# Three edits to a two-block model on one core: who splits the output weights and when, 64-column block products, and key norms turned by transposition

## The chip, the cores and the metric

One Trainium2 chip, and on it one core. The metric is the device time of one execution in microseconds (us): the median of the runs shown.

## The reference, cut to what matters

The kernel computes a chain of layers on a sequence of 256 tokens of width 1024, in float32: a mixer of pooling and gated delta rule, an MLP, a spatial gating mixer, a second MLP, an RWKV-7 mixer, a third MLP, and a last norm. Two places of it are touched by the change.

```python
# first mixer (gated delta rule, 4 heads of width 128, chunks of 64): a unit triangular system per chunk
m = jnp.einsum('bhncd,bhnjd->bhncj', kb, kh) * decay_strict
sol = lax.linalg.triangular_solve(jnp.eye(C) + m, rhs, left_side=True, lower=True)
# RWKV-7 mixer (16 heads of width 64): the keys are scaled by their norm, and the result goes through w_o
kk = kk / jnp.maximum(jnp.sqrt(jnp.sum(kk * kk, axis=-1, keepdims=True)), 1e-12)
y = _wkv7_scan(r_h, heads(decay), k_h, v_h, kk, kk * heads(a))
...
return y @ w_o, v_first          # (256 x 1024) @ (1024 x 1024)
```

## The kernel before, in words

**Products in three parts.** A float32 matrix product of the projections is made of three fast ones. Each operand is split into a high part `h` (a cast to the rounded type `fp32r`) and a low part `l` (what the cast left out), and `mm3` adds `h h`, `h l` and `l h` (L225 to L227). A weight must therefore be loaded, cast and its low part made before its first use. `split` (L213, L217) casts on ScalarE (ACT) and subtracts on VectorE (DVE). With `lo="x"` it calls `rest` instead: ACT writes minus the high part into `l` (L221), and GpSimd (POOL) issues a DMA that adds the loaded weight onto it (L222). Small products inside the mixers are plain float32 matmuls; each shows in the trace as two weight loads and two matmuls, and a transposition as one of each.

**Order.** The library that builds the program orders each engine's queue itself, by its own estimates of durations, so a line's place in a queue isn't its place in the source. In the trace, TensorE (PE) runs matmuls of a later projection ahead of the key-norm matmuls that stand above it. Each queue is then worked off in order: an instruction that waits holds all that stand behind it on its engine. SyncE (SP) issues the weight loads, in the same way.

**First mixer** (`block1`). For two blocks `n` of 128 tokens and four heads, the inverse of a 128x128 triangular matrix is built by elimination in blocks of 16 and three doubling steps `b` = 16, 32, 64. Each step makes `Y = offT^T X` (L793), copies it to SBUF (ACT, L795), makes `Z = U^T Y` (L801) and `ZT = Y^T U` (L806), and adds them to `X` and `U` (DVE, L803 and L808). All are 128x128 per head. Between the steps, `fill()` lets pieces of other projections run.

**RWKV mixer** (`rwkv`). After the k, r and v projections, `scale_ab` (four calls) spreads the inverse key norms to 128x128 tiles (ACT, L1417) and multiplies each by the identity on PE (L1421), which turns it; DVE multiplies by the result (L1423). Then an elimination on DVE, and a scan over four windows `w` of 64 tokens for two halves `hb` of the heads. `step(s, fills)` works on window `s` of half 0 and window `s-1` of half 1: `state`, `solve`, `update`, `output`, each some small matmuls and an ACT copy out of PSUM (L1661, L1671, L1697). `fills` are four lists of other work that is put between them. Among it are `gate_in(n)` (loads `gb`, three DMAs), `gate(n, t)` (PE into `lg`, DVE), `fin(d, n)` (the norm of a finished half, on DVE and ACT, with transpositions into `yh`, `yl` at its end: L1705 to L1718, L246), `out_mm(t, k, first)` (the output product with weight chunk `k`, PE into `ra`), and `w_out`.

**Output weights.** Each call of `w_out` prepares the next of eight chunks `k` of 128 rows of `rwkv_w_o_2`. One load `rwo` of 1 MB holds two chunks. It lies in a "raw" buffer; there are two of these, which `gb`, the v weights ahead of it and the first loads of the third MLP (`m3u`, `m3d`) use too, in turn. Chunks 0 and 1 are split into buffers of the pool `wz` that the v weights used before. The other six go to homes that the scan frees on its way: chunk 2 to the tiles of the gain and of `sq`, 3 and 4 to `lv` (windows 0 and 1 of the scan's matrices), 5 to `EL`, 6 to `mix`, 7 to `lx` (window 2). All eight low parts are made by `rest`.

```python
if homes[k] is None:
    wo.append(split(w, "rwo", "x", of=wz))
else:
    h, l = homes[k]()
    act.copy(h, w)
    rest(l, h, w)
```

Of the kernel before, what the change touches and what calls it, by code (L numbers as in the profile page):

```python
# [10 lines left out]
F32 = mybir.dt.float32  # L11
# [6 lines left out]
P = 128  # L18
T = 256
# [105 lines left out]
def tile_two_blocks(ctx: ExitStack, tc: tile.TileContext, a: dict):  # L125
# [30 lines left out]
    def gps(name):  # L156
        turn[0] += 1
        if turn[0] % 4 < 2:
            return ps(name)
        if turn[1]:  # L160
            return lin(name)
        return acc(turn[0] % 4 - 2, name)[:, :512]
# [306 lines left out]
    def block1():  # L469
        with tc.tile_pool(name="b1", bufs=1) as bp, tc.tile_pool(name="b1s", bufs=2) as bs:  # L470
# [6 lines left out]
            with tc.tile_pool(name="n0", bufs=1) as np_:  # L477
# [20 lines left out]
                for i, (t, n) in enumerate(N_MAJOR if KP.get("um") else T_MAJOR):  # L498
# [3 lines left out]
                    if KP.get("uo") and i in KP["ui"]:  # L502
                        j = len(hl)
# [156 lines left out]
            def fill():  # L660
                n = KP["n"][step[0]]
                step[0] += 1
                for _ in range(n):
                    next(more, None)
# [49 lines left out]
            def v4(q):  # L714
                return q.rearrange("p (h c) -> p h c", h=4)
# [62 lines left out]
            for n in range(2):  # L778
# [7 lines left out]
                    pe.transpose(q[:, h * P:(h + 1) * P], X[:, n, h], ident)  # L786
                act.copy(U[:, n], v4(q))
            fill()
            for b in (16, 32, 64):
                for n in range(2):  # L790
                    q = gps("Y")
                    for h in range(4):
                        pe.matmul(q[:, h * P:(h + 1) * P], lhsT=offT[b][:, n, h], rhs=X[:, n, h],  # L793
                                  start=True, stop=True)
                    act.copy(Y[:, n], v4(q))  # L795
                fill()
                for n in range(2):
                    if b < 64:
                        q = gps("Z")
                        for h in range(4):  # L800
                            pe.matmul(q[:, h * P:(h + 1) * P], lhsT=U[:, n, h], rhs=Y[:, n, h],  # L801
                                      start=True, stop=True)
                        dve.tensor_add(X[:, n], v4(q), X[:, n])  # L803
                    q = gps("ZT")
                    for h in range(4):
                        pe.matmul(q[:, h * P:(h + 1) * P], lhsT=Y[:, n, h], rhs=U[:, n, h],  # L806
                                  start=True, stop=True)
                    dve.tensor_add(U[:, n], v4(q), U[:, n])  # L808
                fill()

            while not turn[1]:
# [329 lines left out]
    def rwkv(fed, early, cols, mu, hcol, hka, laf):  # L1141
        NP, CH = 8, 64
        half = 0.5 * DECAY
        with tc.tile_pool(name="wz", bufs=2) as wz, tc.tile_pool(name="rw", bufs=1) as bp:
# [75 lines left out]
            with tc.tile_pool(name="rwm2", bufs=2) as m2, tc.tile_pool(name="rwm", bufs=1) as mp:  # L1220
# [193 lines left out]
                def scale_ab(c):  # L1414
                    s = slice(2 * c, 2 * c + 2)
                    wide = wd[:, c].rearrange("p (t k n) -> p t k n", t=2, k=4)
                    act.copy(wide, nr[:, :, 4 * c:4 * c + 4].unsqueeze(3).to_broadcast([P, 2, 4, 64]))  # L1417
                    q = ps("nk")
                    for j in range(2):
                        for t in range(2):  # L1420
                            pe.matmul(q[:, j * T + t * P:j * T + t * P + P], rhs=ident, start=True, stop=True,  # L1421
                                      lhsT=wide[:, t, 2 * j:2 * j + 2].rearrange("p k n -> p (k n)"))
                    dve.tensor_tensor(out=tA[:, s], in0=tA[:, s], in1=as2(q.rearrange("p (j t) -> p j t", j=2)),  # L1423
                                      op=ALU.mult)
                    dve.scalar_tensor_tensor(tB[:, s], as2(ta[:, s]), -0.5, tA[:, s], ALU.mult, ALU.mult)
                    tA5 = tA[:, s].rearrange("p k d (e t) -> p k d e t", e=2)
                    EN[KP["tk"][0]].tensor_tensor(out=tA5, in0=tA5, in1=EL5[:, s, :, :, 0:CH], op=ALU.mult)
                    EN[KP["tk"][1]].tensor_tensor(out=tK[:, s], in0=tK[:, s], in1=as4(tt[:, s]), op=ALU.mult)
# [318 lines left out]
                def w_out():  # L1747
                    k = len(wo)
                    if k % 2 == 0:
                        wo_raw.append(load_as(a["rwkv_w_o_2"][0], k * P, f"rwo{k}"))  # L1750
                    w = wo_raw[-1][:, k % 2]
                    if homes[k] is None:
                        wo.append(split(w, "rwo", "x", of=wz))
                    else:
                        h, l = homes[k]()
                        act.copy(h, w)
                        rest(l, h, w)
                        wo.append((h, l))

                def out_mm(t, k, first):  # L1760
# [22 lines left out]
                for _ in c0:  # L1783
                    next(late_fill, None)
                before([(0, 0)])
                both_fill = [some(c1, 2) + some(late_fill, 2)] * 3
                step(0, both_fill + [rest_of(c1) + rest_of(late_fill) + [lambda: v_out(1), lambda: gate_in(0)]])
                yh, yl = xt_tiles("y")
                f00, f01, f10, f11 = [fin(d, n) for d in both for n in both]
                step(1, [[lambda: gate(0, 0)], [lambda: gate(0, 1), lambda: gate_in(1)], [w_out], [w_out]])  # L1790
                step(2, [some(f00) + [lambda: gate(1, 0)], some(f00) + [lambda: gate(1, 1)],
                         some(f00) + [w_out], some(f00)])
                step(3, [some(f01) + [w_out], some(f01) + [w_out], some(f01) + [w_out], some(f01) + [w_out, w_out]])
                ac = [acc(0, "ra0")]
                outs = lambda t, ks, first: [lambda k=k: out_mm(t, k, first) for k in ks]
                step(4, [some(f10) + outs(0, [0], 0), some(f10) + outs(0, [1], 0), [], some(f10) + outs(0, [2], 0)])
# [108 lines left out]
```

## Time and profile before

| What | us |
|---|---|
| median of 3 runs | 1082.83 (1080.8 to 1084.26) |
| the profiled execution's own time | 1082.16 |
| its span, first to last instruction | 1080.4 |

The span is 1.76 us shorter than the profiled execution's time, and that time lies 0.67 us under the median of the runs. PE is the busiest engine by far. A busy share is an average; where PE waits, and where its granted clock is down, is read stretch by stretch. PEld is PE's weight load, which runs beside its matmuls.

### The profile page before, as it was taken

The numbers are of one execution on the slowest core, as the hardware profiler recorded it, in microseconds if no ns is written. First come the engines' busy times: TensorE is split into PE (matmuls) and PEld (weight loads), VectorE is DVE, ScalarE is ACT, GpSimd is POOL, SyncE is SP. The second block draws the span as 40 slices with busy tenths as digits, with TensorE's granted clock in tenths as the row PEclk, the third lists the DMA queues.
The fourth block names the chain that finished last, engine by engine and source line by source line (L and its number), as shares of the span: only waits on it lengthen the run. The fifth ranks groups of instructions, "written<-read, shape, count | busy, mean of one in ns | idle before, by whom it ended". The sixth has DMA issues, their size and how long they took to land.

```text
span 1080.4 us, 18579 instructions
## 1 busy us (share of the span) xinstructions
PE 1043.5 (97%) x7626; PEld 932.3 (86%) x7626; DVE 716.3 (66%) x1201; ACT 567.3 (53%) x840; POOL 59.0 (5%) x94
## 2 busy tenths in 40 slices
PE   8999999999999999999999999999999789999996
PEld 6899878988899999889989998998777569999985
DVE  5989665555658886666685556998936465555565
ACT  5744464454456554555464546864656445444452
POOL 3100000000002000000000001022001100000000
PEclk9999999999999999999999999999999799999999
DMA  8343186555565645556575561456624874566531
GB/s 247 120 157 118 46 314 214 182 181 177 174 198 153 197 155 174 178 166 190 161 248 188 191 192 36 109 148 142 152 50 118 188 221 159 192 195 187 187 134 39
DMA packets 124465, 177.76 MB, mean 165 GB/s; under 512 B 6766, under 2 KB 100955, under 8 KB 124124
## 3 DMA queue, kind: packets, MB, share of 16 engines
q1 hardware_dynamic: 121930, 168.11, 49.0%
q0 software_dynamic: 2304, 8.39, 4.1%
q8 instruction: 60, 0.98, 0.4%
q14 instruction: 25, 0.20, 0.1%
q10 hardware_dynamic: 146, 0.07, 0.0%
HBM read 167.12 MB, written 1.05 MB: 156 GB/s over the span
## 4 chain that ended last, share of the span: by engine, by line
PE 82%; DVE 9%; DMA 4%; ACT 2%; issue 2%; POOL 1%; SPq 0%; ACTq 0%; POOLq 0%; DVEq 0%
PE m3h L227 3%; PE m3h L226 3%; PE m1a L225 3%; PE m3h L225 3%; PE m1a L227 3%; PE m1a L226 3%; PE m1h L226 3%; PE m2h L226 3%; PE m1h L227 3%; PE m2h L227 3%; PE m1h L225 3%; PE m2h L225 3%; PE m2a L225 3%; PE m2a L226 3%; PE m2a L227 3%; PE m3a L225 3%
## 5 line engine op out<-in xcount | busy, mean ns | idle before, releaser
L225 PE MATMUL m3h<-m3xh,m3uh 128*128 128x256 f32 x256 | 72.6, 284 | 1.9 <-ACT m3xh L382 1.9
L227 PE MATMUL m3h<-m3xh,m3ul 128*128 128x256 f32 x256 | 73.0, 285 | 0.5 <-DVE m3ul L217 0.5
L225 PE MATMUL m1h<-m1xh,m1uh 128*128 128x256 f32 x256 | 73.4, 287 | 0.0
L217 DVE TENSOR_TENSOR m3ul<-m3u,m3uh 128x1024 fp32r<-128x1024 f32 x32 | 39.2, 1226 | 51.1 <-ACT m3uh L213 51.1
L226 PE MATMUL m3h<-m3xl,m3uh 128*128 128x256 f32 x256 | 73.0, 285 | 0.0
L226 PE MATMUL m1h<-m1xl,m1uh 128*128 128x256 f32 x256 | 71.8, 281 | 0.2 <-DVE m1xl L385 0.2
L227 PE MATMUL m2h<-m2xh,m2ul 128*128 128x256 f32 x256 | 71.7, 280 | 0.0
L227 PE MATMUL m1h<-m1xh,m1ul 128*128 128x256 f32 x256 | 71.7, 280 | 0.0
L226 PE MATMUL m2h<-m2xl,m2uh 128*128 128x256 f32 x256 | 71.6, 280 | 0.0
L225 PE MATMUL m2h<-m2xh,m2uh 128*128 128x256 f32 x256 | 71.5, 280 | 0.0
L217 DVE TENSOR_TENSOR m1ul<-m1u,m1uh 128x1024 fp32r<-128x1024 f32 x32 | 39.2, 1225 | 45.1 <-ACT m1uh L213 45.0
L213 ACT CAST m3uh<-m3u 128x1024 fp32r<-128x1024 f32 x32 | 33.4, 1047 | 56.5 <-PE m3h L226 50.7
L217 DVE TENSOR_TENSOR m2ul<-m2u,m2uh 128x1024 fp32r<-128x1024 f32 x32 | 39.1, 1225 | 35.8 <-ACT m2uh L213 35.8
L213 ACT CAST m1uh<-m1u 128x1024 fp32r<-128x1024 f32 x32 | 33.7, 1053 | 52.3 <-PE m1h L226 50.5
L213 ACT CAST m2uh<-m2u 128x1024 fp32r<-128x1024 f32 x32 | 33.5, 1050 | 47.9 <-PE m2h L226 45.8
L217 DVE TENSOR_TENSOR m2dl<-m2d,m2dh 128x1024 fp32r<-128x1024 f32 x32 | 39.2, 1225 | 26.1 <-ACT m2dh L213 26.1
L217 DVE TENSOR_TENSOR m3dl<-m3d,m3dh 128x1024 fp32r<-128x1024 f32 x31 | 38.0, 1225 | 24.9 <-ACT m3dh L213 24.9
L217 DVE TENSOR_TENSOR m1dl<-m1d,m1dh 128x1024 fp32r<-128x1024 f32 x31 | 37.9, 1224 | 22.0 <-ACT m1dh L213 22.0
L225 PEld LDWEIGHTS m3h<-m3xh,m3uh 128*128 128x128 f32 x256 | 49.0, 192 | 2.8 <-ACT m3xh L382 2.2
L213 ACT CAST m2dh<-m2d 128x1024 fp32r<-128x1024 f32 x32 | 33.6, 1050 | 33.4 <-PE m2a L227 29.9
L213 ACT CAST m1dh<-m1d 128x1024 fp32r<-128x1024 f32 x31 | 32.5, 1047 | 35.3 <-PE m1a L227 24.4
L213 ACT CAST m3dh<-m3d 128x1024 fp32r<-128x1024 f32 x31 | 32.6, 1052 | 33.4 <-PE m3a L227 31.6
(691 smaller groups left out, 3513.4 us busy)
## 6 DMA issues: line engine op xcount, KB each, us to landing
m1u<-in_w_up_dram SPq DMA_DIRECT2D x16, 1024.0 KB, 5.5
m1d<-in_w_down_dram SPq DMA_DIRECT2D x16, 1024.0 KB, 5.0
m2u<-in_ffn_w_dram SPq DMA_DIRECT2D x16, 1024.0 KB, 6.4
m2d<-in_ffn_w_dram SPq DMA_DIRECT2D x16, 1024.0 KB, 5.2
m3u<-in_ffn_w_dram SPq DMA_DIRECT2D x16, 1024.0 KB, 5.5
m3d<-in_ffn_w_dram SPq DMA_DIRECT2D x16, 1024.0 KB, 5.1
win<-in_w_in_dram SPq DMA_DIRECT2D x10, 1024.0 KB, 5.3
sv<-in_sgu_w_in_dram SPq DMA_DIRECT2D x8, 1024.0 KB, 5.8
```

The lines of the kernel that those rows point to most:

```text
L213: act.copy(hv, src)
L217: lo.tensor_tensor(out=lv, in0=src, in1=hv.bitcast(F32), op=ALU.subtract)
L225: pe.matmul(out, lhsT=lh, rhs=rh, start=first, stop=False)
L226: pe.matmul(out, lhsT=lh, rhs=rl, start=False, stop=False)
L227: pe.matmul(out, lhsT=ll, rhs=rh, start=False, stop=last)
```

## The change

Four things are edited.

- `w_out` makes the low part of every chunk by one DVE subtraction in place of `rest` (`split` with its default, or `tensor_sub`). POOL's DMAs and ACT's second pass for these eight chunks are gone; the `rest` of the v weights stays.
- The calls of `w_out` are moved. Chunks 0 and 1 go from `step(1)` to the end of `step(0)`, right behind `gate_in(0)` and so ahead of `gate_in(1)`; chunk 2 from `step(2)` to `step(1)`; chunk 3 from `step(3)` to the end of `step(2)`; 4 to 7 stay in `step(3)`.
- The block products take 64 moving columns per head. `part` picks those columns of `X`, `Y` or `U` that are not zero or change, in pieces of `b` columns; the results lie packed in 256 columns of PSUM. The stationary operand stays 128x128. POOL now clears the other half of `Y` in each step.
- `scale_ab` uses a transposition where it multiplied by the identity.

```diff
             for b in (16, 32, 64):
                 for n in range(2):
+                    pool.memset(part(Y[:, n], b, 1), 0.0)
                     q = gps("Y")
                     for h in range(4):
-                        pe.matmul(q[:, h * P:(h + 1) * P], lhsT=offT[b][:, n, h], rhs=X[:, n, h],
-                                  start=True, stop=True)
-                    act.copy(Y[:, n], v4(q))
+                        pe.matmul(col64(q, h), lhsT=offT[b][:, n, h], rhs=part(X[:, n], b, 0, h), start=True, stop=True)
+                    act.copy(part(Y[:, n], b, 0), packed(q, b))
                 fill()
                 for n in range(2):
                     if b < 64:
...
-                            pe.matmul(q[:, h * P:(h + 1) * P], lhsT=U[:, n, h], rhs=Y[:, n, h],
-                                      start=True, stop=True)
-                        dve.tensor_add(X[:, n], v4(q), X[:, n])
+                            pe.matmul(col64(q, h), lhsT=U[:, n, h], rhs=part(Y[:, n], b, 0, h), start=True, stop=True)
+                        dve.tensor_add(part(X[:, n], b, 0), packed(q, b), part(X[:, n], b, 0))
...
-                        pe.matmul(q[:, h * P:(h + 1) * P], lhsT=Y[:, n, h], rhs=U[:, n, h],
-                                  start=True, stop=True)
-                    dve.tensor_add(U[:, n], v4(q), U[:, n])
+                        pe.matmul(col64(q, h), lhsT=Y[:, n, h], rhs=part(U[:, n], b, 1, h), start=True, stop=True)
+                    dve.tensor_add(part(U[:, n], b, 1), packed(q, b), part(U[:, n], b, 1))
...
-                            pe.matmul(q[:, j * T + t * P:j * T + t * P + P], rhs=ident, start=True, stop=True,
-                                      lhsT=wide[:, t, 2 * j:2 * j + 2].rearrange("p k n -> p (k n)"))
+                            pe.transpose(q[:, j * T + t * P:j * T + t * P + P],
+                                         wide[:, t, 2 * j:2 * j + 2].rearrange("p k n -> p (k n)"), ident)
...
-                        wo.append(split(w, "rwo", "x", of=wz))
+                        wo.append(split(w, "rwo", of=wz))
                     else:
                         h, l = homes[k]()
                         act.copy(h, w)
-                        rest(l, h, w)
+                        dve.tensor_sub(l, w, h.bitcast(F32))
...
-                step(0, both_fill + [rest_of(c1) + rest_of(late_fill) + [lambda: v_out(1), lambda: gate_in(0)]])
+                step(0, both_fill + [rest_of(c1) + rest_of(late_fill) + [lambda: v_out(1), lambda: gate_in(0), w_out, w_out]])
...
-                step(1, [[lambda: gate(0, 0)], [lambda: gate(0, 1), lambda: gate_in(1)], [w_out], [w_out]])
-                step(2, [some(f00) + [lambda: gate(1, 0)], some(f00) + [lambda: gate(1, 1)],
-                         some(f00) + [w_out], some(f00)])
-                step(3, [some(f01) + [w_out], some(f01) + [w_out], some(f01) + [w_out], some(f01) + [w_out, w_out]])
+                step(1, [[lambda: gate(0, 0)], [lambda: gate(0, 1), lambda: gate_in(1)], [w_out], []])
+                step(2, [some(f00) + [lambda: gate(1, 0)], some(f00) + [lambda: gate(1, 1)], some(f00), some(f00) + [w_out]])
+                step(3, [some(f01) + [w_out], some(f01) + [w_out], some(f01), some(f01) + [w_out, w_out]])
```

## Rows read from the trace of the kernel before

**Rows 1.** The page's first part: busy time of each engine, its share of the span, and its instructions.

```profile
PE 1043.5 (97%) x7626; PEld 932.3 (86%) x7626; DVE 716.3 (66%) x1201; ACT 567.3 (53%) x840; POOL 59.0 (5%) x94
```

**Rows 2.** Windows of the end of the RWKV mixer: each stretch and its length, busy time (instructions) of PE, PEld, DVE, ACT and POOL, then the granted clock of PE as a share of 2.4 GHz, the DMA share and GB/s.

```profile
821.00:833.00 12.00, 11.66 (x153) 10.03 (x152) 8.10 (x23) 7.71 (x11) 1.75 (x2) 1.00 0.58 131
833.00:848.00 15.00, 9.38 (x86) 6.83 (x85) 5.86 (x17) 8.37 (x11) 1.73 (x2) 1.00 0.81 176
848.00:867.00 19.00, 17.41 (x83) 12.79 (x81) 7.21 (x18) 9.35 (x14) 3.46 (x4) 0.55 0.81 193
867.00:878.40 11.40, 9.78 (x44) 7.29 (x44) 9.13 (x21) 3.46 (x6) 0.00 (x0) 1.00 0.79 253
878.40:889.00 10.60, 7.70 (x34) 5.45 (x34) 6.55 (x14) 6.15 (x16) 0.00 (x0) 1.00 0.72 228
```

**Rows 3.** The chain that ended last, in the stretch from 800 to 900 us, its longest pieces: start, us, what.

```profile
838.10 9.53 DMA lv<-rwo
859.87 10.59 DMA lx<-rwo
877.87 7.01 DMA m3u<-in_ffn_w_dram
```

**Rows 4.** The timeline around it: start, us, engine, line, what it writes from what it reads, and the idle time before it with what ended it.

```profile
840.13 0.92 PE L1693 MATMUL PD<-tBK,lx 128*64 128x64 f32 x13
845.23 1.04 ACT L1756 CAST lv<-rwo 128x1024 fp32r<-128x1024 f32 x1 [6.56 <-DMA rwo<-in_rwkv_w_o_dram]
847.67 0.50 PE L226 MATMUL ra<-lv,yh 128*128 128x512 f32 x1 [3.44 <-DMA lv<-rwo]
849.15 1.19 ACT L1697 COPY tBK<-PD 64x512 f32<-64x512 f32 x2
866.60 0.58 ACT L1697 COPY tBK<-PD 64x512 f32<-64x512 f32 x1 [0.67 <-PE PD L1693]
877.06 0.66 PE L246 MATMUL yt<-ident,tBK 128*128 128x128 f32 x4 [0.94 <-DVE tBK L1718]
```

**Rows 5.** What SP, which issues the loads, waited for between 740 and 900 us: us in total, times, longest. L184 loads `rwo` (and `m3d`), L1561 is the first load of a `gb`.

```profile
SPq L1561 <- DMA wvl<-wv: 30.5, 2, 16.7
SPq L184 <- DMA rwol<-rwo: 11.6, 1, 11.6
SPq L184 <- DMA lv<-rwo: 10.1, 1, 10.1
```

**Rows 6.** Costs of one split: groups between 805 and 890 us with total and mean ns (ACT's cast, ACT's second pass, a DVE subtraction of the same shape), and the last line of the tile `rwo`, the time to landing of the DMAs that read or write it.

```profile
L1756 ACT CAST wo<-rwo 128x1024 fp32r<-128x1024 f32 x3 | 3.1, 1043 | 0.0
L221 ACT ACTIVATE wo<-wo 128x1024 fp32r<-128x1024 f32 x3 | 3.1, 1049 | 0.0
L217 DVE TENSOR_TENSOR m3ul<-m3u,m3uh 128x1024 fp32r<-128x1024 f32 x3 | 3.7, 1224 | 3.4 <-ACT m3uh L213 3.4
DMA to landing us min/median/max: 5.4/9.1/11.3
```

**Rows 7.** The timeline of what `gb` and the first `rwo` stand next to: the end of the v projection, SP's issues, the first matmul of the gate that needs the second `gb`; the last row is the last line of the tile `gb`, the time to landing of its loads.

```profile
793.46 0.33 SPq L1561 DMA_DIRECT2D gb<-in_rwkv_g_lora_b_dram  x1
804.62 0.40 PE L227 MATMUL v<-wvh,mvl 128*128 128x512 f32 x1
814.46 33.66 SPq L184 DMA_DIRECT2D rwo<-in_rwkv_w_o_dram  x4
815.02 0.50 PE L225 MATMUL lg<-lgbh,gfh 128*128 128x512 f32 x1
DMA to landing us min/median/max: 2.6/3.5/4.5
```

**Rows 8.** The block products of the first mixer: the three groups of matmuls (total us, mean ns), then a window over them (columns as in Rows 2).

```profile
L793 PE MATMUL Y<-X,off 128*128 128x128 f32 x48 | 6.3, 275 | 0.0
L806 PE MATMUL ZT<-U,Y 128*128 128x128 f32 x48 | 6.3, 277 | 0.0
L801 PE MATMUL Z<-Y,U 128*128 128x128 f32 x32 | 4.3, 277 | 0.0
90.80:108.00 17.20, 17.17 (x145) 16.71 (x146) 14.88 (x36) 9.39 (x17) 0.22 (x2) 1.00 0.27 88
```

**Rows 9.** Timeline, weight loads merged: eight of the products, eight of a product with 16 moving columns, sixteen with a 64x64 stationary operand and 64 moving columns, sixteen of the key norms, four of a transposition.

```profile
94.26 0.97 PEld L801 LDWEIGHTS Z<-Y,U 128*128 128x128 f32 x8
63.18 0.98 PEld L764 LDWEIGHTS fold<-cc,ab 128*128 128x128 f32 x8
811.04 1.00 PEld L1669 LDWEIGHTS Ud<-xx,TT 64*64 64x64 f32 x16 [0.75 <-ACT xx L1661]
728.18 1.86 PEld L1421 LDWEIGHTS nk<-ident,ly 128*128 128x128 f32 x16 [0.33 <-ACT ly L1417]
831.07 0.47 PEld L246 LDWEIGHTS yt<-ident,tBK 128*128 128x128 f32 x4
```

**Rows 10.** POOL, by form: a clearing of 512 elements per partition.

```profile
L1471 POOL MEMSET TT<- 32x512 f32 x4 | 2.1, 522 | 0.2
```

**Rows 11.** What DVE waited for around the key norms, and windows from there to the end of the v projection (columns as in Rows 2).

```profile
DVE tAR L1423 <- PE nk L1421: 0.4, 2, 0.2
726.00:734.00 8.00, 7.88 (x68) 7.64 (x66) 7.15 (x14) 4.42 (x9) 1.28 (x1) 1.00 0.42 133
742.00:805.00 63.00, 61.93 (x665) 49.15 (x663) 43.65 (x97) 37.30 (x66) 9.54 (x11) 0.95 0.56 133
```

More of the change, by code (lines that the diff above doesn't have):

```diff
@@ L788, in block1, with part, packed, col64 @@
             fill()
+            def part(x, b, u, h=None):
+                if h is None:
+                    return x.rearrange("p h (g u c) -> p (h g) u c", u=2, c=b)[:, :, u]
+                return x[:, h].rearrange("p (g u c) -> p g u c", u=2, c=b)[:, :, u]
+            def packed(q, b):
+                return q[:, :256].rearrange("p (g c) -> p g c", c=b)
+            def col64(q, h):
+                return q[:, h * 64:h * 64 + 64]
             for b in (16, 32, 64):
                 for n in range(2):
+                    pool.memset(part(Y[:, n], b, 1), 0.0)
                     q = gps("Y")
                     for h in range(4):
-                        pe.matmul(q[:, h * P:(h + 1) * P], lhsT=offT[b][:, n, h], rhs=X[:, n, h],
-                                  start=True, stop=True)
-                    act.copy(Y[:, n], v4(q))
+                        pe.matmul(col64(q, h), lhsT=offT[b][:, n, h], rhs=part(X[:, n], b, 0, h), start=True, stop=True)
+                    act.copy(part(Y[:, n], b, 0), packed(q, b))
                 fill()
```

## Prediction, made before the changed kernel ran

> **What bounds the kernel now.** I read the page's first part for the engine that fills the span, then windows over the stages that the diff touches, then the chain that ended last, the timeline and SP's waits in the stage where PE is not full. PE is busy 97% of the span [rows 1], so over most of the kernel only PE's own work counts, and an edit on another engine is worth something only where PE stops. In the first mixer's block products PE stops for 0.03 us of 17.2 [rows 8], between the key norms and the end of the v projection for little more than 1 us of 63 [rows 11]. The end of the RWKV mixer is another matter. Up to 833 PE is full (11.66 of 12 us). From 833 to 878.4 it is idle for 5.62 + 1.59 + 1.62 = 8.8 us, and for the 19 us after the first gap its granted clock is 0.55 of 2.4 GHz, mostly the 1.2 GHz level [rows 2]. The reader is to see the two losses together: 17.41 us of work at 0.55 would be 9.6 us at the full clock, so 7.8 us go to the clock.
>
> What ends the waits is read from the chain: a DMA onto `lv` for 9.53 us, one onto `lx` for 10.59 us [rows 3]. These are the accumulating DMAs of `rest`. They cost in three ways. PE waits for a low part (3.44 us at 847.67). ACT's cast for `lv` waits 6.56 us for its load `rwo`, and the scan's copies out of PSUM stand behind it in ACT's queue: the matmuls into `PD` of 840.13 are copied only from 849.15 on [rows 4]. And the load is late because SP waits 11.6 and 10.1 us until such DMAs have let go of the two raw buffers [rows 5].
>
> **The change part by part.**
>
> *Output weights.* Removed: eight ACT passes of 1.05 us and eight POOL DMAs, whose landing takes up to 11.3 us. Added: eight DVE subtractions of 1.22 us [rows 6]. A chunk's low part then follows its cast by some 1.3 us in place of about ten, and a raw buffer comes free that much sooner. POOL has nothing else to do there, so its part costs nothing and frees nothing. Moving chunks 0 and 1 to the end of `step(0)` lets the first `rwo` take the raw buffer that the second `gb` takes now, at 793.46, in place of 814.46 [rows 7]. The later loads follow as gates and splits let go of buffers, and by my count of buffers all eight chunks are split by about 842. The third MLP's first loads stand behind them and also move forward.
>
> How much comes back? The floor of PE for the work between 833 and 878.4 at the full clock is 9.38 + 9.58 + 9.78 = 28.7 us against 45.4, so the ceiling is 16.7 us. DVE does 5.86 + 7.21 + 9.13 = 22.2 us there [rows 2] and gets five more subtractions (the first three fall earlier), 28.3 us in all: it becomes as full as PE. Two in-order engines that feed each other through ACT never pack perfectly, so I take the idle share of PE from the neighbours. As dense as 821 to 833 (2.8% idle): 28.7/0.972 = 29.6, a gain of 15.8. As dense as 867 to 878.4 (14%): 33.4, a gain of 12. As loose as 878.4 to 889, where the chain and the load of `m3u` rule (27%): 39.5, a gain of 5.9 [rows 2]. I take 13, between the first two and nearer to the second, because DVE is now full too and the last chain stays: from the last copy at 866.60 to the transposition at 877.06 [rows 4], 10.5 us, during which PE has other output products to do. What is late next is this chain, and behind it the 7 us load of `m3u` [rows 3], which waits for the mixer's memory as before. I count nothing for it either way.
>
> *Block products.* 128 records of PE (48 + 48 + 32) [rows 8] go from 128 to 64 moving columns. The stationary operand stays 128x128, and its load sets the pace: eight records take 0.97 us with 128 moving columns and 0.98 us with 16 [rows 9]. So 64 columns give nothing, and I take 0. The bounds: if only the 64-column rows count, where a stationary operand of 64 goes with it, a record takes 1.00/16 = 0.063 in place of 0.121 us, and 128 x 0.058 = 7.4 us would come back. On the other side, six POOL clearings of 256 elements cost at most the 0.52 us of one with 512 [rows 10] each, 3.1 us if all lay on the path. I expect them hidden: each needs only the previous step's products done and has DVE's addition and the next `Y` products as cover. Shorter additions and copies on DVE and ACT are worth nothing while PE is full. A moving operand in pieces of 16 columns has no row of its own here; at twice a record's time it would cost 128 x 0.12 = 15 us, for which nothing in the rows speaks; I keep it as part of the slower side.
>
> Here the Trainium skill speaks on both sides. "TensorE: Matmul & The Clock Gate", section "Back-to-back issue gap", has 134 cycles for 128 columns and about 60 for 64, by which these products would shorten by some half, 7 us. The section "LDWEIGHTS (loading the stationary operand)" has P/1.2 ns for P columns of stationary operand, 107 ns for 128 of them whatever moves, by which they shorten by nothing. The two rows of eight records above agree with the second.
>
> *Key norms.* 32 records become 16, for a transposition is one record: four take 0.47 us, sixteen key-norm records 1.86 us [rows 9]. That is 16 x 0.117 = 1.9 us of PE. PE is full there, but so is DVE (7.15 of 8 us), which waits only 0.4 us for these products [rows 11]; the DVE work behind them cannot start earlier by more than that. What PE saves it can use up to the end of the v projection at 804.62, where it is full for 61.93 of 63 us. I take 1.0, between 0.4 and 1.9.
>
> *The sum.* 13 + 0 + 1 = 14 us, against the profiled execution's 1082.16: 1068.2, rounded to **1068**. The median of the runs is 0.67 us above that execution, which is inside the rounding that I allow. Some 0.3%, 3.2 us, is about what a measurement of this kernel can tell from no change.
>
> **The rivals.**
>
> 1. *The chain rules* (DVE and the last norm). DVE is at 28.3 us of a floor of 28.7, and every subtraction that waits for its cast holds the scan's additions and the norms behind it. If the stage stays as loose as 878.4 to 889, the gain is 5.9 + 1 and the time 1075. For it: the 10.5 us from the last copy to its transposition are DVE work, and in a compressed stage more of it collides. Against: most of DVE's idle time there was waiting for ACT, which loses eight passes.
>
> 2. *Fewer columns do pay.* The products give 7.4 us more: 1061. For it are only rows with a smaller stationary operand; against it the 16-column row.
>
> 3. *Slower: the second `gb` comes late.* It now follows the first `rwo`, whose second half can be split only when the v projection has let go of its buffer, 805.0. With a cast and a subtraction that is 807.3; 2.6 to 4.5 us for the load make it 811.8; its own smaller split, at most as long as a full one, ends by 814.1. PE reads it first at 815.02 [rows 6, 7]. The margin is about 1 us. A late `gb` stops PE in order, and a gap there can bring the clock down as it did at 848, which cost 7.8 us. To eat all 14 us the gap itself must then be 6.2 us, so `gb` must be split after 821. I see nothing that makes it 7 us late, unless the library puts the casts of `rwo` badly into ACT's queue.
>
> 4. *No effect*: the library orders the queues anew, and gains here are lost elsewhere; within 3 us of before.
>
> **How the numbers follow.** My forecast (a gain of 9 to 19 us) gets 0.67; rival 1, with a gain from 4 to 9, 0.16; rival 2, 0.05; rival 3, 0.06; rival 4, 0.06. Ordered by time, rival 2 lies below 1063, the forecast from 1063 to 1073, rival 1 up to 1078. A range from 1060 to 1077 leaves out rivals 3 and 4 and the ends of rivals 1 and 2, together under 2 in 10. The forecast's own range is 1063 to 1073. Faster by over 0.3% is the forecast, rivals 1 and 2 and a small part of the rest: 0.89. Within 0.3%: 0.06. Slower: 0.05.
>
> **What the profile of after would show.** Right: no DMA on `rwol`, `wo`, `lv` or `lx` in the chain between 830 and 880; SP's waits for such DMAs gone; the granted clock near 1.0 throughout the stage; the last norm's transposition at about 863 in place of 877. The block products keep about 0.12 us per record, with ACT and DVE shorter beside them; the key norms take half their time. Wrong would be: eight block records in clearly less than 0.97 us; PE idle for more than a fifth of the stage with DVE behind it (rival 1); a wait for `gb` or `lgbh` ahead of the second gate (rival 3). A change in the three MLPs' steady stretches would mean that I missed something.

## The result, and the profile after

The changed kernel takes 1070.07 us (median of 4 runs, 1069.54 to 1071.7) against 1082.17 for the kernel before beside it: a ratio of 0.9886, 95% interval 0.987 to 0.9902. By the ratio that is 12.3 us less; the medians differ by 12.1. Its profiled execution took 1069.54 us, with a span of 1067.8. The forecast was 1068. The size came out; two of the reasons did not, as the experiments show.

First the page's busy times of the changed kernel (columns as in [rows 1]), then windows of the end of its RWKV mixer (columns as in [rows 2]). The stretches are the same in time, so the work in them is somewhat later work.

```profile
PE 1036.1 (97%) x7610; PEld 927.3 (87%) x7610; DVE 719.5 (67%) x1209; ACT 558.7 (52%) x832; POOL 53.8 (5%) x92
```

```profile
821.00:833.00 12.00, 9.74 (x139) 7.86 (x137) 10.09 (x25) 7.36 (x12) 0.00 (x0) 1.00 0.43 139
833.00:848.00 15.00, 13.20 (x117) 10.75 (x118) 11.08 (x22) 8.09 (x12) 0.00 (x0) 0.77 0.31 100
848.00:867.00 19.00, 18.09 (x103) 13.72 (x103) 14.76 (x39) 4.62 (x8) 0.00 (x0) 1.00 0.31 112
867.00:878.40 11.40, 9.88 (x51) 7.62 (x49) 6.50 (x17) 6.92 (x19) 0.00 (x0) 1.00 0.70 231
```

PE stops for 2.3 + 1.8 + 0.9 us up to 867, and the granted clock dips once, to 0.77; before, it was 0.55 for 19 us. DVE does 42.4 us in these four stretches, against 30.3 in [rows 2]. What PE waits for now is DVE. The timeline of the changed kernel (columns as in [rows 4]):

```profile
832.82 1.23 DVE L1766 TENSOR_TENSOR lv<-rwo,lv 128x1024 fp32r<-128x1024 f32 x1 [0.32 <-ACT lv L1765]
833.97 0.68 DVE L1727 TENSOR_TENSOR tBK<-tBK,V 128x512 f32<-128x512 f32 x1
834.80 0.86 PE L246 MATMUL yt<-ident,tBK 128*128 128x128 f32 x4 [3.69 <-DVE tBK L1727]
```

A subtraction stands ahead of the last operation of the first output norm, and PE's transposition behind it waits 3.69 us. SP's waits between 800 and 880 us no longer name a DMA onto a low part of the output weights. Before, four of them did, two in [rows 5] and these two:

```profile
SPq L184 <- DMA lx<-rwo: 11.3, 1, 11.3
SPq L178 <- DMA wo<-rwo: 10.5, 1, 10.5
```

In the changed kernel, the longest wait and three of the others:

```profile
SPq L178 <- PE yt L246: 14.2, 1, 14.2
SPq L184 <- DVE lx L1766: 10.5, 1, 10.5
SPq L1570 <- DVE rwol L217: 10.3, 1, 10.3
SPq L1570 <- DMA rwo<-in_rwkv_w_o_dram: 4.6, 1, 4.6
```

The next table has the lengths of four stretches, each from the first start of one product, or the last of `v`, to the first or last start of another, in one profiled execution of each kernel that has some parts of the change (the changed one twice). They show where the kernels differ; the times of whole runs scatter by several microseconds. "Gap" is PE's idle time at the `AB` products. The kernels are named by what they have: W the output weights (Ws the subtraction alone, Wm the moved calls alone), P the 64-column products, N the transposed key norms.

| kernel | first `Y` to first `m1h` | first `k` to last `k` | gap | first `k` to last `v` | last `v` to first `m3a` | ratio of times |
|---|---|---|---|---|---|---|
| before | 56.4 | 34.8 | 1.0 | 124.4 | 98.6 | 1 |
| P | 54.1 | 36.1 | 0.7 | 127.2 | 99.7 | 0.9989 |
| N | 54.6 | 34.7 | 2.9 | 126.5 | 99.6 | 1.001 |
| Ws | 55.0 | 34.7 | 0.9 | 125.9 | 91.2 | 0.991 |
| Wm | 56.6 | 34.8 | 0.6 | 125.7 | 90.3 | 0.9899 |
| W | 56.8 | 34.8 | 0.8 | 125.6 | 87.4 | 0.9896 |
| W + P | 54.1 | 36.0 | 0.7 | 127.6 | 86.8 | 0.9904 |
| W + N | 56.2 | 34.8 | 2.8 | 127.8 | 85.5 | 0.9897 |
| W + P + N (after) | 54.1 | 36.3 | 2.7 | 127.8 | 85.0 | 0.9886 |
| after, again | 54.1 | 36.6 | 2.8 | 129.4 | 85.1 | 0.9886 |

Each row is one execution, and those of P and Wm took 4.0 and 4.6 us more than the median of their kernel. Each length also holds what the clock took in that execution. The time spent at the lower of the two levels (1.2 GHz) can be estimated as 2 x (1 - granted share) x length, added up over short windows. From 120 to 155 us it is 3.4 or 3.5 us in the kernel before, Wm, W and W + N, and 0 in the others. From 722 to 806 us it is 6.9 us in the kernel before, 13.5 and 13.7 in W + N and in the second profile of the changed kernel, and 10.2 to 10.4 in the other seven. At half the clock, 3.4 us there make a length 1.7 us longer. Ws has 10.3 us there in place of 6.9, though its output weights are loaded only from 814 us on. So 1.7 us in the first or the fourth column of lengths can be the clock of one execution and not an edit.

### The profile page after: what moved, and what is told of

It is laid out like the page before. It is cut to its first block, busy times and chain, and to the rows that moved or that the text cites. A ratio compares the mean times of both kernels' runs of the same rounds, so it can differ in the third digit from the quotient of the medians.

```text
span 1067.8 us, 18548 instructions
## 1 busy us (share of the span) xinstructions
PE 1036.1 (97%) x7610; PEld 927.3 (87%) x7610; DVE 719.5 (67%) x1209; ACT 558.7 (52%) x832; POOL 53.8 (5%) x92
## 4 chain that ended last, share of the span: by engine, by line
PE 85%; DVE 9%; ACT 2%; issue 2%; POOL 0%; DMA 0%; SPq 0%; ACTq 0%; POOLq 0%; DVEq 0%
PE m1a L225 3%; PE m3h L226 3%; PE m3h L227 3%; PE m1a L227 3%; PE m1a L226 3%; PE m3h L225 3%; PE m1h L226 3%; PE m2h L226 3%; PE m1h L227 3%; PE m2h L227 3%; PE m2h L225 3%; PE m1h L225 3%; PE m2a L225 3%; PE m2a L226 3%; PE m2a L227 3%; PE m3a L226 3%
## 5 line engine op out<-in xcount | busy, mean ns | idle before, releaser
L225 PE MATMUL m2a<-m2dh,m2fh 128*128 128x512 f32 x128 | 50.1, 392 | 0.0
```

The costliest lines, as they stand in the source:

```text
L225: pe.matmul(out, lhsT=lh, rhs=rh, start=first, stop=False)
```

## The experiments

### Each part alone

**The output weights alone**, both halves of the edit:

```diff
-                        wo.append(split(w, "rwo", "x", of=wz))
+                        wo.append(split(w, "rwo", of=wz))
...
-                        rest(l, h, w)
+                        dve.tensor_sub(l, w, h.bitcast(F32))
...
-                step(0, both_fill + [... lambda: v_out(1), lambda: gate_in(0)]])
+                step(0, both_fill + [... lambda: v_out(1), lambda: gate_in(0), w_out, w_out]])
...
```

> The kernel before with the output-weight edits alone (DVE subtraction in place of the ACT pass and the accumulating DMA, and the moved calls). Theory (the stage's 11.8 us come from these edits and nothing else): 1082.2 - 11.8 - 1.8 for the start of the third MLP = 1068.6, accepted from 1067 to 1071; the matmuls of the mixer's start (m1's first, the k projection) stand where they stood before. Rival (part of it came from the earlier or later start of the mixer in the changed kernel): 1072 or more.

Measured: 1071.19 us, ratio 0.9896 (0.988 to 0.9912). It misses the accepted bounds by 0.2 us (the kernel before took 1083.24 beside it), but carries 11.3 of the 12.3 us, and the stretch behind the last `v` falls to 87.4 us. By the times, what the two other edits add to it can't be told from nothing.

**The block products alone** (`part`, `packed` and `col64` as in the change, nothing else).

> The kernel before with the 64-column block products alone. Theory A (my forecast, only the pitch of PE counts): eight records keep 0.97 us and the time stays at 1082 +- 0.8. Theory B (the first matmul of m1, which starts 2.3 us earlier in the changed kernel, does so because DVE and ACT are shorter here): 1079.9, with the gap of PE ahead of m1x shorter and the gain in front of 148 us kept to the end. Rival C (64 columns pay on PE): 1075, with eight records in 0.5 us.

Measured: 1080.96 us, ratio 0.9989 (0.9973 to 1.0005). The time can't be told from no change. Rival C is out, since the pitch of PE stayed. Theory B holds in the profile: `m1h` starts 54.1 us after the first `Y`. PE's wait for the residual, in the waits of the kernel before and then of this one:

```profile
PE m1x L379 <- DVE res L343: 1.9, 1, 1.9
```

```profile
PE m1x L379 <- DVE res L343: 0.5, 1, 0.5
```

In the table the stretch is 54.1 us in all four rows with P and 54.6 to 56.8 in the six without. But the two of these six in which the clock stays up there, N and Ws, show 54.6 and 55.0. So at the same clock the edit is worth 0.5 to 0.9 us in this place, and the rest of its 2.3 us is the clock, which falls in the four others. That the shorter wait is what keeps the clock up isn't shown: in N and Ws it stayed up behind waits of 1.6 and 2.0 us. In the k projection the four rows with P need 36.0 to 36.6 us and the six others 34.7 or 34.8. Windows there, of the kernel before and then of this one:

```profile
697.00:701.00 4.00, 2.90 (x24) 2.56 (x22) 4.00 (x6) 2.29 (x5) 0.00 (x0) 1.00 0.00 0
701.00:705.00 4.00, 4.00 (x24) 4.00 (x24) 3.72 (x8) 2.51 (x7) 2.14 (x2) 0.60 0.55 154
705.00:709.00 4.00, 4.00 (x35) 4.00 (x34) 4.00 (x9) 3.41 (x4) 0.56 (x1) 0.97 0.40 113
```

```profile
697.00:701.00 4.00, 2.90 (x18) 2.56 (x16) 3.25 (x5) 2.29 (x7) 0.00 (x0) 0.75 0.02 4
701.00:705.00 4.00, 4.00 (x20) 4.00 (x21) 3.66 (x7) 1.42 (x4) 2.41 (x2) 0.50 0.84 238
705.00:709.00 4.00, 4.00 (x33) 4.00 (x33) 4.00 (x9) 3.13 (x4) 0.30 (x1) 0.90 0.08 24
```

PE stops for the same 1.1 us in both, and the stretch at the lower clock around it is longer in the second: 18 + 20 + 33 instructions in the place of 24 + 24 + 35. So the 1.3 us lost at 700 us are more than half of the 2.3 won at 145. Why the clock stays low for longer there, 550 us behind the edit, no run shows.

**The key norms alone** (`pe.transpose` in place of `pe.matmul` on the identity).

> The kernel before with the transposed key norms alone. Theory (my forecast): 1081.2, the saving of PE arrives by half. Rival (the 3.4 us that the changed kernel loses between the k projection and the end of v come from this edit, through PE's waits around the AB products and the slower clock behind them): 1083 to 1085.6.

Measured: 1083.59 us, ratio 1.001 (0.9995 to 1.0025): not to be told from no change. My forecast of 1.0 us less (0.9991) lies outside the interval, and the rival's range begins at about what was measured. PE's timeline around the `AB` products, of the kernel before and then of this one:

```profile
738.88 1.17 PE L1482 MATMUL AB<-tAR,tBK 64*32 64x32 f32 x111
741.02 0.34 PE L1482 MATMUL AB<-tAR,tBK 64*32 64x32 f32 x17 [0.97 <-issue]
```

```profile
736.77 1.20 PE L1482 MATMUL AB<-tAR,tBK 64*32 64x32 f32 x114
740.87 0.32 PE L1482 MATMUL AB<-tAR,tBK 64*32 64x32 f32 x14 [2.90 <-issue]
```

The burst of tiny products comes 2.1 us earlier, which is the saving of the transpositions and a little more, and its last 14 start at the same time as before. In between PE waits for nothing that the profile names ("issue"). The table has this gap at 2.7 to 2.9 us in every kernel with N and at 0.6 to 1.0 in every kernel without.

### One part left out of the change

**Without the transpositions.**

> The changed kernel with the key norms as before (32 matmuls on the identity). Theory (transpositions worth 1.0 us): 1071.1. Rival (they cost time in this place): 1066.7 to 1069, faster than the changed kernel, and the loss between 678 and 806 gone. A third possibility is that the loss comes from the 2.3 us earlier start, so that it stays: 1070 to 1071 with the same slow stretch of the clock in the k projection.

Measured: 1072.15 us, ratio 0.9904 (0.9888 to 0.992). The gap is gone (0.7 us), and the time isn't better for it. Alone the edit seems to cost 1.1 us and inside the change to bring 1.9, both within the intervals: by the times it is worth nothing that can be told. The stretch from `k` to `v` stays at 127.6, so that the loss there isn't this edit's alone, as the third possibility had it. Against the 125.6 to 125.9 of Ws, Wm and W, both W + P and W + N show some 2 us more, of which 1.7 in W + N are the clock's by the estimate above. They don't add: with both it is 127.8 and 129.4 in two profiles of one kernel.

**Without the 64 columns.**

> The changed kernel with 128-column block products. If the 64 columns are worth nothing: 1070 +- 1.5, as the changed kernel. If the shorter DVE and ACT work beside them is worth the 2.3 us at the end of the first mixer: 1072.4, with the first m1h some 56.5 us after the first Y product in place of 54.1.

Measured: 1071.76 us, ratio 0.9897 (0.9872 to 0.9921), between the two expectations and not to be told from either; the first `m1h` is 56.2 us behind the first `Y`, as the second had it. Windows of this kernel and then of the changed one, in its second profile, at the end of the first mixer:

```profile
138.00:143.00 5.00, 2.80 (x12) 1.82 (x11) 3.25 (x4) 1.28 (x2) 0.00 (x0) 0.90 1.02 409
143.00:148.00 5.00, 5.00 (x25) 4.15 (x24) 2.77 (x9) 3.04 (x10) 0.00 (x0) 0.76 0.61 198
```

```profile
138.00:143.00 5.00, 3.62 (x16) 2.45 (x17) 3.69 (x5) 2.20 (x6) 0.00 (x0) 1.00 1.03 397
143.00:148.00 5.00, 5.00 (x38) 4.64 (x37) 4.47 (x14) 4.31 (x13) 0.00 (x0) 1.00 0.63 181
```

PE stops for 2.2 us in the first and 1.4 in the second, and the clock falls only in the first. The first residual addition stands behind the split of an `m1u` whose load is issued at 132.73 in the one and 132.16 in the other, so it starts half a microsecond earlier (140.56 in place of 141.03), and the clock adds to that. What in the shorter additions and copies moves that load was not traced further.

### The two halves of the output-weight edit

**The subtraction at the old places** (the first two pieces of the first diff).

> The kernel before with VectorE's subtraction for the output weights, the calls where they were. Theory (the accumulating DMAs are what costs, by their landing and the raw buffers that they hold): most of the 12.9 us between the end of v and m3a comes back here, 1070 to 1074; no DMA on lv, lx or wo in the chain between 830 and 880. Rival (the calls' places decide, because a raw buffer is first free there): 1077 or more, with ACT still waiting for rwo loads that were issued late.

**The moved calls, low parts still by `rest`** (the last piece of it).

> The kernel before with the calls moved as in the changed kernel, the low parts still by the ACT pass and the accumulating DMA. Theory (the DMAs cost): 1079 to 1083, SP's waits for DMA onto rwol and lv still there. Rival (the places decide): 1070 to 1074. A third case: slower than before, up to 1087, since the second gb then waits for an accumulating DMA of 10 us to let go of its raw buffer.

Measured: the subtraction alone 1073.25 us, ratio 0.991 (0.9881 to 0.9939); the moves alone 1071.46, ratio 0.9899 (0.9871 to 0.9926). For the first kernel the theory held, for the second the rival. Either half brings most of the gain: 7.4 and 8.3 us in the stretch behind `v`, both together 11.2 (W) to 13.6 (after). By the whole times the moves alone can't be told from both halves (0.9896). What the two share shows in SP's timeline, here the issues of the last `rwo` loads (start, and the us from the first of them to the last) of the subtraction alone, the moves alone and the changed kernel:

```profile
814.59 21.09 SPq L184 DMA_DIRECT2D rwo<-in_rwkv_w_o_dram  x4
```

```profile
818.59 19.86 SPq L184 DMA_DIRECT2D rwo<-in_rwkv_w_o_dram  x3
```

```profile
814.84 15.38 SPq L184 DMA_DIRECT2D rwo<-in_rwkv_w_o_dram  x3
```

The last load goes out at 836, 838 and 830 us; before it was 814.46 + 33.66 = 848 [rows 7]. The one half makes each raw buffer come free sooner, the other lets the first load start sooner (797.1 and 795.9 us, in the two kernels with the moves). With the moves alone the accumulating DMAs are all still there, as its waits show, and two windows:

```profile
SPq L184 <- DMA lx<-rwo: 10.7, 1, 10.7
SPq L178 <- DMA wo<-rwo: 10.4, 1, 10.4
SPq L184 <- DMA lv<-rwo: 10.2, 1, 10.2
PE ra L226 <- DMA lx<-rwo: 1.3, 1, 1.3
```

```profile
833.00:848.00 15.00, 13.32 (x117) 10.40 (x117) 7.97 (x20) 10.68 (x15) 2.60 (x3) 0.77 0.85 190
848.00:867.00 19.00, 15.47 (x83) 11.14 (x82) 9.89 (x24) 6.67 (x10) 1.72 (x2) 0.91 0.70 174
```

SP waits 10 us for three of them, PE only 1.3 us for one, and the clock is 0.91 where it was 0.55. The landing time as such wasn't the price; what fits these rows is that the low parts came too late with it. The third case, a second `gb` held up, didn't come: it was issued at 815.1, and PE shows no wait for it.

**Two low parts by DMA again.** The changed kernel, with

```diff
-                        dve.tensor_sub(l, w, h.bitcast(F32))
+                        if k in (3, 4):
+                            rest(l, h, w)
+                        else:
+                            dve.tensor_sub(l, w, h.bitcast(F32))
```

> The changed kernel with the low parts of the output-weight chunks 3 and 4 by the ACT pass and the accumulating DMA again, the other six by VectorE's subtraction. Theory (what is left of the stage is VectorE, whose subtractions stand before the last operation of the first output norm): PE's wait of 3.7 us ahead of the first output transposition falls to 1.5 us or less, the clock behind it stays at 1.0, and the time is 1066 to 1069. Rival (the two DMAs hold the raw buffers again): SP waits some 10 us for DMA onto lv, the later chunks come late, and the time is 1070 to 1074.

Measured: 1071.56 us, the same as the changed kernel beside it. PE's wait ahead of the first transposition:

```profile
PE yt L246 <- DVE gv L1722: 2.7, 1, 2.7
SPq L178 <- DMA lv<-rwo: 10.0, 1, 10.0
```

With two of DVE's subtractions gone from there, the wait falls from 3.7 to 2.7 us and no further, and the stretch stays at 85.4 us. So most of that wait isn't made by those two subtractions. My theory fell; the rival's time came, and SP's waits with it.

### The gap at the `AB` products

In the changed kernel the first two weight tiles of the v projection are split earlier than before, since ACT and DVE are through with the key norms sooner, and their accumulating DMAs (`wvl`) are issued at 734.5 and 739.0 instead of 738.2 and 745.6. Does PE wait for its instructions behind them?

**All eight low parts of `wv` by GpSimd.** One letter code in the table of choices, from the DMA to POOL:

```diff
-    'rv': 'x,x,x,x,x,x,x,x',
+    'rv': 'p,p,p,p,p,p,p,p',
```

> The changed kernel with the low parts of the eight v-projection weight tiles subtracted by GpSimd in place of the ACT pass and the accumulating DMA (some 2 MB less through the DMA engines between 733 and 800). Theory (the 2.7 us in which PE waits for nothing the profile shows, at the AB products, are an instruction load that meets this traffic): the gap falls to 1 us or less and the time to 1068. Rival (the gap comes from the order of the PE queue alone, 112 tiny products in a row): the gap stays at 2 to 3 us, the time at 1070. A third case: GpSimd's subtraction is so slow (its 128x512 operations take 1.3 to 1.9 us, so 2.6 to 3.7 us each) that the v projection waits for it: over 1073.

Measured: 1078.8 us, ratio 0.9963 (0.9946 to 0.9979). The gap falls to 0.3 us, as the theory had it, and yet the kernel is 8 us slower than the changed one. The subtractions take 2.4 to 2.9 us, but the v projection doesn't wait for them. What is longer is DVE's work: PE's waits for DVE between 680 and 820 us rise from 1.3 to 7.3 us. The timeline of POOL and DVE at one of them:

```profile
764.13 2.45 POOL L217 TENSOR_TENSOR wvl<-wv,wvh 128x1024 fp32r<-128x1024 f32 x1 [8.75 <-issue]
764.38 2.47 DVE L1598 TENSOR_TENSOR sq<-hT 128x238 f32<-128x238 f32 x1
```

An operation of 0.40 us ends with POOL's, after 2.47. The two lines of the solve that it belongs to take 14.5 + 14.0 us of DVE up to the end of `v`, against 10.4 + 9.9 in the changed kernel; By the estimate above, the time at the lower clock grows too, from 10.4 us (722 to 806) to 23.8 (722 to 816). Six more microseconds of waits and half of 13.4, less 2.4 for the gap, are 10.3 us, about the 9.4 by which the stretch from `k` to `v` is longer; which of them brings on which was not tried. (The DMAs taken away move 4.2 MB by the profile, not 2.) "SBUF — State Buffer" of the Trainium skill, section "SBUF: two separate sides", says that VectorE and GpSimd share a pair of ports, and that of a GpSimd operation that reads SBUF and a VectorE operation with two SBUF inputs, the one that starts first holds the pair for its whole length. The trace agrees with that.

**The first two by VectorE.** `'rv': 'd,d,x,x,x,x,x,x'`.

> The changed kernel with the first two of the eight v-projection low parts subtracted by VectorE in place of the ACT pass and the accumulating DMA. Theory (the 2.7 us of PE at the AB products are a late instruction load behind this DMA traffic): the gap falls under 1 us; the two subtractions cost VectorE 2.4 us in a stretch where it is full for 6.5 of 7 us, so that the time is 1068 to 1071. Rival (the gap comes from the order of the PE queue): gap 2 to 3 us, time 1071 to 1073.

Measured: 1065.7 us (1064.63 to 1067.66), ratio 0.9835 (0.9802 to 0.9868), 5.9 us below the changed kernel beside it: faster than both kernels, and better than the theory had it. The stretch from `k` to `v` is 124.1 us, 3.7 less than in the first profile of the changed kernel: 2.0 are the gap, and by the estimate above 1.7 are the clock (6.9 us at the lower level in place of 10.4). PE's timeline of this kernel, then the DMA queues in two microseconds of it and of the changed kernel (packets, MB, share of 16 engines; q0 carries the accumulating DMAs, q1 the loads, q8 the instructions), 737 to 738 here and 738 to 739, 739 to 740 there:

```profile
737.90 1.18 PE L1491 MATMUL AB<-tAR,tBK 64*32 64x32 f32 x112
739.83 0.33 PE L1491 MATMUL AB<-tAR,tBK 64*32 64x32 f32 x16 [0.75 <-issue]
q1 hardware_dynamic: 6, 0.01, 22.8%
q8 instruction: 1, 0.02, 6.3%
```

```profile
q0 software_dynamic: 35, 0.13, 96.3%
q1 hardware_dynamic: 2, 0.00, 5.7%
q1 hardware_dynamic: 105, 0.22, 82.7%
q8 instruction: 1, 0.02, 5.8%
q0 software_dynamic: 13, 0.00, 1.1%
```

The burst starts at the same time in both, 737.88 and 737.90. Here the DMA engines are nearly free, the instruction block comes in the microsecond from 737, and the last 16 products run at 739.83. There the accumulating DMA fills the engines up to 739, the block comes between 739 and 740 beside a load, and they run at 741.73. That it is PE's block is inferred, since the trace doesn't say whose it is. But in windows of 0.1 us of all fourteen profiled executions the last of these products start 2.2 to 2.8 us behind such a block, whether the gap is 0.3 or 2.9 us.

**The same without the transpositions**, to see whether the two subtractions pay by themselves.

> The changed kernel with VectorE's subtraction for the first two v-projection low parts and with the key norms as before (32 matmuls on the identity). Theory (the two subtractions pay because they remove the gap of PE at the AB products, which only the kernels with transpositions have at 2.7 us): without the transpositions the gap is 0.7 us already, the subtractions give 1 us or less, and the time is 1070 to 1072. Rival (they pay by themselves, because raw buffers and ACT come free earlier, and the gap is a small part): 1066 to 1068.

Measured: 1074.59 us, ratio 0.9929 (0.9912 to 0.9946). They pay nothing by themselves: against the kernel with W and P alone (0.9904, up to 0.992) it is rather slower, beyond what the theory had, though the intervals just meet. In the profiled executions the stretch from the first `k` to the last `v` is 128.2 us here and 124.1 with the transpositions, the shortest of all. Of these 4.1 us, 1.9 are PE's saving by the transpositions, 0.6 the gap (1.3 us here), and by the estimate above 1.7 the clock (10.2 us at the lower level in place of 6.9). So the saving seems to arrive once the instruction block isn't kept from PE; that rests on one execution of each. The times say more, 8.9 us, and the ratios, each with the kernel before beside it, some 10; the profiled executions differ by 5.5, and the rest isn't explained.

**The changed kernel again**, beside the kernels with two low parts by DMA and with two by VectorE.

> The changed kernel as it is, beside the two that follow, which change one thing of it each. Theory (the 2.3 us that its profile gained at the end of the first mixer and the 3.4 us that it lost in the start of the RWKV mixer are partly the clock of that one execution): 1070 +- 1, with the first m1h 54.1 us after the first Y product again, and the stretch from the first k product to the last v product between 126 and 128 us.

Measured: 1071.56 us, ratio 0.9886 (0.9853 to 0.9919). The first stretch is 54.1 us again and the gap 2.8, so neither was a matter of one execution. The stretch from `k` to `v` was 129.4 us, outside what I expected: there PE waits a second time in the k projection, for 1.7 us, and the clock falls behind that wait only. Behind the first, of 1.1 us, it stays at 1.00. So P's four rows share the longer k projection, but not one cause for it.

## Why the prediction was right, point by point

- **What bounds the stage**: right. PE idle and the clock behind it came back together. The stretch from the last `v` to `m3a` is 98.6 to 99.7 us in the three kernels without W and 85.0 to 87.4 in the five rows with both halves of it. In this stretch PE is idle for 13.2 us before and 7.0 after, and the estimated time at the lower clock falls from 20.5 to 6.8 us. The 6.2 us and half of the 13.7 make some 13 of the 13.6 us gained.
- **Output weights, 13 us**: measured 11.3 us by the time of this edit alone, 11.2 to 13.6 by the stretch. The size is right; the mechanism was half right. I put the loss on the accumulating DMAs. The kernel that keeps all eight of them and only starts the loads earlier gains 8.3 us in that stretch. What failed is the step from "the chain names a DMA of 10 us" to "the gain is the DMA's": what fits all three kernels is the lateness of the last loads, which either half mends, and the two don't add (7.4 and 8.3 give 11 to 14). For the subtraction alone, sooner low parts and sooner loads were not told apart.
- **The clock near 1.0 throughout, the chunks split by 842, the last transposition at 863**: 0.77 in one stretch, the last subtraction ending at 847.3, 865.17. DVE became what PE waits for at one place, as rival 1 had it, but only there. The sign that no DMA onto a low part stands in the chain between 830 and 880 us came true.
- **The start of the third MLP, counted as nothing**: the changed kernel shows 1.8 us less from `m3h` to `m3a` (14.9 to 13.1). The kernels with P alone and N alone, which have the old output stage, show 13.4 and 13.3. With the moved calls alone it is 14.9 again. What these kernels win here they lost ahead of `m3h`, so only the whole stretch up to `m3a` is to be read.
- **Block products, 0**: right for the reason given, PE's pitch. In the changed kernel:

```profile
95.02 0.97 PEld L812 LDWEIGHTS Z<-Y,U 128*128 128x128 f32 x8
```

```profile
90.80:108.00 17.20, 17.15 (x151) 17.00 (x152) 10.34 (x29) 7.99 (x17) 1.47 (x6) 1.00 0.07 28
```

  Eight records keep their 0.97 us [rows 9] with half the columns; PE is full for 17.15 of 17.20 us as it was for 17.17 [rows 8]; rival 2 is out. By "LDWEIGHTS (loading the stationary operand)" of "TensorE: Matmul & The Clock Gate" in the Trainium skill a weight load takes as long as the stationary operand has columns, here 128. The trace agrees that the moving columns don't matter; a record takes 0.121 us here, where the section's formula gives 0.107. What failed is the sentence that shorter additions and copies are worth nothing while PE is full. DVE went from 14.88 to 10.34 us there, and 35 us later, where PE isn't full, `m1h` starts earlier, by 0.5 to 0.9 us at the same clock and by 2.3 against the profile of before. In the k projection 1.3 us are lost again, so the time doesn't tell.
- **Key norms, -1.0**: wrong. The PE saving came as worked out (16 weight loads in 0.94 + 0.46 + 0.46 us in place of 32 in 3.72), but the work behind it ran into a wait that I had not priced, the longer gap. I had read the windows up to `v` as full and asked only what DVE would allow; the 1.0 us of "issue" at these products, which was there before, I passed over. The two windows of [rows 11] leave out the 8 us in which it lies:

```profile
734.00:742.00 8.00, 7.03 (x286) 6.08 (x285) 6.29 (x10) 2.11 (x2) 1.04 (x1) 1.00 0.32 81
```

- **Rival 3** (a late second `gb`): its load did wait 10.3 us for a split of `rwo` and 4.6 us for a `rwo` load, and was issued at 811.2, but PE's matmuls show no wait for it. The margin of about 1 us was used up: the split of this `gb` ended at 815.73, and PE's weight load waited for it beside a matmul.

```profile
815.79 0.19 PEld L226 LDWEIGHTS lg<-lgbl,gfh 128*128 128x128 f32 x1 [0.29 <-DVE lgbl L217]
```

The errors partly cancel: 2.3 us gained up to `m1h`, 3.4 lost from `k` to `v`, 11.8 gained up to `m3h` for the 13 forecast, 1.8 gained behind it. By the estimate above, 1.7 of the first 2.3 are the clock of that execution of the kernel before, so that the forecast came out as near as this is in part luck.

## What to carry to other kernels

A long DMA at the end of a wait says that something is late, not that the DMA is what to remove: first ask when its chain of buffers could have begun. Time that an edit saves on a full PE is kept only if what follows can start earlier too, so look at the first stretch behind it where PE waits, for "issue" as much as for a semaphore, and at what transfers the earlier start puts beside it. Lengths of stretches over many kernels can show effects of 1 to 2 us that whole times don't, but only beside the clock of each execution: one kernel's two profiles differ by 1.6 us in one stretch.

## What was not expected of the hardware

- 128 products of 0.011 us each seem to outrun PE's supply of instructions: 109 to 114 of them run in 1.15 to 1.20 us (1.65 in the kernel with GpSimd's subtractions), and then PE waits 0.3 to 1.3 us for the rest, and 2.7 to 2.9 when an accumulating DMA of 0.5 MB occupies the DMA engines at that moment (share 0.92 and over). Taking that DMA away brought the gap down both times; that it is the instructions which come late is inferred from the block on queue q8.
- A subtraction of 128x1024 on GpSimd, 2.45 us, holds up one of VectorE's for as long (2.47 in place of 0.40 us); in the kernel with eight of them the last `v` comes 137.2 us behind the first `k`, against 127.8.
- The same idle 1.1 us of PE goes with some 3 or some 7 us at the lower clock (from the granted shares of the three windows above, 2 x (1 - share) x 4 us each: 3.2 + 0.2 and 2.0 + 4.0 + 0.8), in kernels that differ only 550 us earlier, and with none in the second profile of the changed kernel (1.00 from 697 to 709 us).
